# A hybrid encoder layer with product-key experts: the stores of spread weights cut into four pieces, and one row rate for the whole first product

## The chip, the cores and the metric

The kernel runs on one core of a Trainium2 chip. What is measured is the device time of one execution in microseconds (us); the median of the runs shown is compared. The core has a matmul engine (PE, with its weight loads PEld), a vector engine (DVE), a scalar engine (ACT), GpSimd (POOL) and SyncE (SP). SP starts nearly all the plain transfers here, in the order of its own stream, and POOL starts the gathers by index. All transfers share 16 DMA engines.

## The reference

One layer over 1024 tokens of width 1024: a mixer with two groups (RG-LRU and S5), then a product-key retrieval of experts (PEER), then a norm. The change lies in PEER, cut here to what matters:

```python
def block(xb):                                   # 128 tokens
    q = (xb @ wq).reshape(128, 8, 256)           # 8 heads
    s1, s2 = q[..., :128] @ k1.T, q[..., 128:] @ k2.T
    v1, i1 = top_k(s1, 16); v2, i2 = top_k(s2, 16)
    sc, cidx = top_k(v1[..., :, None] + v2[..., None, :], 16)   # of 256 pairs
    e = i1[cidx // 16] * 128 + i2[cidx % 16]     # expert number, 0 .. 16383
    g = softmax(sc)
    act = gelu(einsum('thkd,td->thk', u_tab[e], xb))
    return einsum('thk,thkd->td', g * act, v_tab[e])
```

So each token uses 8 x 16 = 128 of the 16384 experts; u_tab and v_tab are 16384 x 1024 each.

## The kernel before, in words

The eight blocks of 128 tokens are treated in two ways. Five blocks (ND = 5, TD = 640 tokens) are *dense*: the kernel multiplies the 640 tokens with all the experts and weighs the result with a matrix G that holds a token's weight where it chose an expert and zero elsewhere. Three blocks are *gathered*: for each of the 128 experts of a token, POOL fetches the row of u_tab (later of v_tab) by index (`ask`, one gather of 128 rows, 512 KB, a "row" below), and DVE makes one product with it (`row<-row,xg` for u, `hb<-row,act,hb` for v). That is 3 x 256 = 768 rows, taken in order, eight buffers deep.

The dense way has a first product (`first`): for a tile of 128 experts, `ap` = u tile x 640 tokens, in two halves of 320 tokens, each 24 matmuls (every operand is split in a high and a low part: `uh`, `ul`). ACT applies gelu into the tile `aa`, and the 128 x 640 result is stored to DRAM (`A_d<-aa`, 320 KB), to be read back later as `hr`. `ahead` makes 97 such tiles, 194 halves; its buffers are two pairs `uh`/`ul`, and three `aa`. The load of the next u tile is `ur<-in_uT` (512 KB). After them `dense` runs the second product, with the rest of the rows in between; its order is written out by hand.

While `ahead` runs, `choose` finds the experts of the dense blocks (top-k on DVE) and `build` spreads their weights into G: for each group of four tokens, DVE makes the one-hots `ohA` and one part of `ohB`, ACT the rest of `ohB`, PE multiplies them (`gp<-ohB,ohA`), and `flush` copies the result into a buffer `gs` with ACT. One group belongs to one half: 160 groups follow the first 24 halves. A buffer `gs` collects GT = 32 tokens, eight groups. When it is full, `flush` stores it: G_d is laid out by expert tile, so the store of 2 MB writes 128 x 32 runs of 512 bytes. There are two `gs` buffers and 20 such stores. Of the last one, the 64 KB that the first weights load needs (`gt<-G_d`, `weights(0)`) goes first, and the rest (`rest`) in `prologue`, the piece of code that prepares `dense`.

Four things set the order. `Merge`, a planner, runs these generators and always takes the one that is earliest by its own costs. The gathers have a gate: a row may be planned only while `mg.units < allow[0]`; `allow` starts at FIRST, and after LEAD = 23 halves grows by STEP for each half (one value up to half 151, another after it). Then the tile framework sorts each engine's stream again by its own estimate of what is ready, so what the planner wrote is not yet the stream. And SP's stream is a queue: a transfer whose semaphore is not there, or for which the queue has no room, holds all behind it.

Profile lines: everything recorded through the planner has line L146. Before the change the G stores are L1235, the loads of `ur` L1351 (L1537 in `dense`), the stores of `aa` L1449, the loads of `hr` L1381, of `vr` L1385, of `gt` L1486, the gathered block's `hb<-H_d` L1323 and its result `out_dram<-hb` L1346. After the change all but the G stores are three lines further down.

Of the kernel before, what the change touches and what calls it, by code (L numbers as in the profile page):

```python
# [18 lines left out]
P = 128  # L19
# [9 lines left out]
def bc(ap, pos, n):  # L29
    shape = list(ap.shape)  # L30
    v = ap.unsqueeze(pos)
    shape.insert(pos, n)
    return v.to_broadcast(shape)
# [934 lines left out]
TD = ND * P  # L968
HALF = TD // 2
TG = NG * P  # L970
JC = 4
NA = 97
GT = 32
ROWS = 8
PACE = 2.0
FIRST, STEP, KT, LEAD = 64, (1.55, 2.1), 2, 23


def peer(tc, a, cst, pools, h, nx, mg):


    nc = tc.nc
# [9 lines left out]
    G_d = dr.tile([P // JC, P, TD, JC], F32, name="G_d")  # L992
# [202 lines left out]
    rest = []  # L1195
# [28 lines left out]
    def build():  # L1224
        last = None

        def flush():
            gs, b, t4, p_ = last
            S.activation(gs[:, :, t4 % GT:t4 % GT + 4].rearrange("p j t q -> p t j q"),
                         p_.rearrange("p (t j q) -> p t j q", t=4, q=JC), AF.Copy)  # L1230
            if t4 % GT == GT - 4:
                t0 = b * P + t4 + 4 - GT

                def store(js):
                    nc.sync.dma_start(G_d[js, :, t0:t0 + GT].rearrange("j p t q -> p j (t q)"),  # L1235
                                      gs[:, js].rearrange("p j t q -> p j (t q)"))
                if t0 + GT < TD:
                    store(slice(0, P // JC))
                else:
                    store(slice(0, 1))  # L1240
                    weights(0)
                    rest.append(lambda: store(slice(1, P // JC)))
                mg.dma(GT * 64)
        for b, t4 in [(b, t4) for b in dblocks for t4 in range(0, P, 4)]:
            if t4 == 0:
                if f"k{b}" not in mg.flags:
                    yield f"k{b}"
                kt = kts.pop(b)
            yield lambda: steps[0] >= LEAD + groups[0] or "ahead" in mg.flags
            if t4 % GT == 0:  # L1250
                gs = pk2.tile([P, P // JC, GT, JC], F32, name="gs", tag="gs")
            p_ = pb("gp")
            A = pk2.tile([P, 4, P], F32, name="ohA", tag="ohA")
            B = pk2.tile([P, 4, P], F32, name="ohB", tag="ohB")
            V.tensor_tensor(A, bc(iota, 1, 4), bc(kt[:, 0, t4:t4 + 4], 2, P), ALU.is_equal)
            for e in range(4):
                t = t4 + e
                if e:
                    S.activation(B[:, e], iota, AF.Abs, bias=kt[:, 3, t:t + 1])
                else:  # L1260
                    V.tensor_scalar(B[:, e], iota, kt[:, 1, t:t + 1], kt[:, 2, t:t + 1], ALU.is_equal, ALU.mult)
            for e in range(1, 4):
                t = t4 + e
                S.activation(B[:, e], B[:, e], AF.Relu, bias=kt[:, 2, t:t + 1], scale=kt[:, 4, t:t + 1])
            yield lambda: steps[0] >= LEAD + groups[0] + 1 or "ahead" in mg.flags
            for e in range(4):
                PE.matmul(p_[:, e * P:(e + 1) * P], A[:, e], B[:, e], start=True, stop=True)
            if last:
                flush()
            last = gs, b, t4, p_  # L1270
            groups[0] += 1
            yield
        flush()
        mg.flag("g")
        yield
# [97 lines left out]
    class Tile:  # L1373
# [4 lines left out]
        def load_h(self):  # L1378
            if self.hr is None:
                self.hr = ph1.tile([P, TD], F32, name="hr", tag="hr", bufs=3)  # L1380
                nc.sync.dma_start(self.hr, A_d[self.j])  # L1381

        def load_v(self):
            self.vr = pu.tile([P, D], F32, tag="raw", name="vr", bufs=3)
            nc.sync.dma_start(self.vr, a["v"][:, self.j])  # L1385
# [30 lines left out]
    def tile(c, n):  # L1416

        if c >= nch:
            return None
        if (c, n) not in TL:  # L1420
            TL[c, n] = Tile(c * JC + (0, 1, 3, 2)[n])
        return TL[c, n]
# [53 lines left out]

    pace[0] = PACE
    mg.add([(0.0, build()), (0.0, choose()), (1.0, ahead())])
    mg.run([], until="k")
    pools.close("pk")  # L1480
# [3 lines left out]
    def weights(c):  # L1484
        gts[c] = pgg.tile([P, TD, JC], F32, name="gt", tag="gt")
        nc.sync.dma_start(gts[c], G_d[c])  # L1486
# [47 lines left out]
    def load_u(c):  # L1534
        if c < nch:
            raw_u[c] = pu.tile([P, 8, P], F32, tag="raw", name="ur", bufs=3)
            nc.sync.dma_start(raw_u[c], a["uT"][tile(c, 2).j])  # L1537
# [10 lines left out]
    def prologue():  # L1548
        now = [tile(0, n) for n in range(JC)]

        def split_v(n):
            now[n].load_v()
            mg.at(mg.dma(512))
            yield
            now[n].high_v()
            now[n].low_v()
            yield

        def weighted(n):
            now[n].turn()  # L1560
            now[n].weigh()
            yield

        def split_h(n):
            now[n].high_h()
            now[n].low_h()
            yield
        for n in (0, 1):
            yield from split_v(n)
        load_h(0, 0)  # L1570
        load_h(0, 1)
        rest.pop()()
        yield lambda: made[0] >= NA - 2
        for n in (0, 1):
            yield from weighted(n)
            yield from split_h(n)
            if n == 0:
                load_h(0, 3)
        yield from split_v(2)
        load_v(0, 3)  # L1580
        yield from weighted(3)
        yield "ahead"
        yield from weighted(2)
        yield from split_h(2)
        load_h(1, 0)
        load_h(1, 1)
        load_u(2)
        weights(1)
        load_v(1, 0)
        mg.flag("pro")  # L1590

    mg.run([(0.5, prologue())], until="pro")
    share[:] = [0.0]
    assert len(mg.ths) == 1
# [237 lines left out]
```

## Time and profile before

| | |
|---|---|
| median of 3 runs | 2627.03 us (2619.6 to 2630.09) |
| profiled execution | 2629.31 us, span 2627.5 us |
| PE busy | 2502.6 us (95%) |
| DVE busy | 2364.6 us (90%) |
| ACT busy, POOL busy | 1333.2 us, 1118.6 us |
| moved by DMA | 753.30 MB, 287 GB/s over the span |
| G stores | 20 of 2 MB (the last in two parts), L1235, first started at 745.4 us, last at 1466.9 us |
| copies into gs (one for each group) | 160, from 713.8 to 1465.9 us |
| second product begins | about 1516 us |

Times are from the start of the span. The busy shares are means over stages with different limits, so they are read here by stage: the front and the queries to about 680 us, the first product with the spreading of weights from there to about 1466 us, eleven more halves to 1516 us, and then the second product. The profiled execution stands 2.3 us above the median of the runs.

### The profile page before, as it was taken

Reading aid. Unit: us, or ns where it says so; the run is one execution under the profiler, and the core shown is the slowest. Engines: PE = TensorE matmul, PEld = TensorE weight load, DVE = VectorE, ACT = ScalarE, POOL = GpSimd, SP = SyncE. Lnnn points to the kernel's source line nnn. Section 1 sums busy time; section 2 is a strip of 40 time slices with the busy share of each in tenths; the row PEclk is TensorE's granted clock in tenths of the full one; section 3 lists DMA queues with packets and bytes.
Section 4 is the critical chain, followed back from the end, with each engine's and each line's share of the span. In section 5 each row is a group of like instructions: output and inputs, shape, how many; then the busy total and the mean of one; then the engine's idle time right before and its main releaser. Section 6 shows DMA issues by size and latency. Waiting matters only on the chain.

```text
span 2627.5 us, 40651 instructions
## 1 busy us (share of the span) xinstructions
PE 2502.6 (95%) x14623; PEld 2266.1 (86%) x14623; DVE 2364.6 (90%) x4556; ACT 1333.2 (51%) x2402; POOL 1118.6 (43%) x777
## 2 busy tenths in 40 slices
PE   7998999998999999999979999999999999999997
PEld 6776888998999999999979988888888888888885
DVE  7898659998999999999976399999989999999997
ACT  5566434332387777877856543333343434333342
POOL 0000000254455574546765065545545666555550
PEclk9999999998999999999989999999999999999998
DMA  5113124587899999999999699999999999999993
GB/s 177 35 41 105 65 91 134 189 280 284 285 327 354 342 346 325 344 318 343 399 375 378 210 328 359 349 362 353 350 328 349 349 355 356 351 350 353 354 359 116
DMA packets 302538, 753.30 MB, mean 287 GB/s; under 512 B 28928, under 2 KB 127424, under 8 KB 297600
## 3 DMA queue, kind: packets, MB, share of 16 engines
q0 software_dynamic: 110592, 402.70, 41.9%
q1 hardware_dynamic: 186048, 337.85, 36.6%
q10 hardware_dynamic: 5696, 10.15, 1.2%
q8 instruction: 115, 1.88, 0.3%
q14 instruction: 87, 0.71, 0.1%
HBM read 663.44 MB, written 85.98 MB: 285 GB/s over the span
## 4 chain that ended last, share of the span: by engine, by line
PE 60%; DVE 25%; DMA 7%; issue 5%; ACT 2%; POOL 1%; ACTq 0%; SPq 0%; DVEq 0%; POOLq 0%
PE vp L146 26%; PE ap L146 18%; PE total L146 7%; DMA A_d<-aa 3%; DVE hb L146 3%; DVE row L146 3%; PE wop L146 3%; DVE ul L146 2%; PE gp L146 2%; DVE oh L146 2%; DVE ohA L146 2%; PE qp L146 2%; DVE ix L146 1%; DMA xq<-in_x_dram 1%; DVE v L146 1%
## 5 line engine op out<-in xcount | busy, mean ns | idle before, releaser
L1287 POOL DMA_INDIRECT row<-in_peer_u_dram,idx x384 | 561.0, 1461 | 952.9 <-DVE scv L146 474.5
L1287 POOL DMA_INDIRECT row<-in_peer_v_dram,idx x384 | 554.8, 1445 | 465.2 <-DVE hb L146 314.3
L146 PE MATMUL ap<-xDl,uh 128*128 128x320 f32 x2048 | 651.5, 318 | 37.7 <-ACT aa L146 36.1
L146 PE MATMUL ap<-xDh,ul 128*128 128x320 f32 x2048 | 637.6, 311 | 5.1 <-DVE ul L146 5.1
L146 PE MATMUL ap<-xDh,uh 128*128 128x320 f32 x2048 | 637.1, 311 | 0.0
L146 DVE SCALAR_TENSOR_TENSOR hb<-row,act,hb 128x1024 f32<-128x1024 f32 x384 | 491.1, 1279 | 4.8
L146 DVE CUSTOM_DVE_ANT_0 row<-row,xg 128x1024 f32<-128x1024 f32 x384 | 456.6, 1217 | 17.3 <-DMA row<-in_peer_u_dram,idx 15.7
L146 PEld LDWEIGHTS ap<-xDl,uh 128*128 128x128 f32 x2048 | 389.5, 190 | 41.6 <-ACT aa L146 38.2
L146 PE MATMUL vp<-vl,hh 128*128 128x512 f32 x1024 | 401.7, 392 | 10.8 <-DVE h L146 8.6
L146 PE MATMUL vp<-vh,hl 128*128 128x512 f32 x1024 | 401.1, 392 | 0.0
L146 PE MATMUL vp<-vh,hh 128*128 128x512 f32 x1024 | 399.9, 390 | 0.0
L146 PEld LDWEIGHTS ap<-xDh,ul 128*128 128x128 f32 x2048 | 389.7, 190 | 7.0 <-DVE ul L146 5.8
L146 PEld LDWEIGHTS ap<-xDh,uh 128*128 128x128 f32 x2048 | 389.0, 190 | 0.0
L146 ACT ACTIVATE gq<-gt 128x640 f32<-128x640 f32 x128 | 175.1, 1368 | 318.7 <-DVE hr L146 254.7
L146 PEld LDWEIGHTS vp<-vl,hh 128*128 128x128 f32 x1024 | 193.4, 189 | 52.4 <-DVE h L146 9.4
L146 PEld LDWEIGHTS vp<-vh,hh 128*128 128x128 f32 x1024 | 193.4, 189 | 41.2
L146 PEld LDWEIGHTS vp<-vh,hl 128*128 128x128 f32 x1024 | 193.4, 189 | 39.0
L146 ACT ACTIVATE ohB<-ohB,kt 128x128 f32<-128x128 f32 x480 | 202.0, 487 | 0.0
L146 ACT ACTIVATE aa<-ap 128x320 f32<-128x320 f32 x194 | 84.4, 436 | 212.1 <-PE ap L146 165.3
L146 DVE TENSOR_TENSOR ul<-ur,uh 128x1024 fp32r<-128x1024 f32 x128 | 155.7, 1217 | 38.0 <-ACT uh L146 38.0
L146 DVE TENSOR_TENSOR h<-h,vp 128x1024 f32<-128x1024 f32 x128 | 155.5, 1215 | 28.0 <-PE vp L146 27.1
L146 PE MATMUL gp<-ohB,ohA 128*128 128x128 f32 x1280 | 170.3, 276 | 9.3 <-DVE ohB L146 7.0
(444 smaller groups left out, 4484.7 us busy)
## 6 DMA issues: line engine op xcount, KB each, us to landing
ur<-in_uT_dram SPq DMA_DIRECT2D x128, 512.0 KB
vr<-in_peer_v_dram SPq DMA_DIRECT2D x128, 512.0 KB
gt<-G_d SPq DMA_DIRECT2D x32, 1280.0 KB
G_d<-gs SPq DMA_DIRECT2D x19, 2048.0 KB
A_d<-aa SPq DMA_DIRECT2D x96, 320.0 KB
hr<-A_d SPq DMA_DIRECT2D x96, 320.0 KB
wqr<-in_wq_dram SPq DMA_DIRECT2D x31, 512.0 KB
row<-in_peer_u_dram,idx POOLq DMA_INDIRECT x384
```

What stands on the lines that cost most here:

```text
L146: return fn(*args, **kw)
L1287: G.indirect_dma_start(out=r, out_offset=None, in_=a["peer_v" if at >= P else "peer_u"], in_offset=bass.IndirectOffsetOnAxis(ap=idx[n][:, ...
```

## The change

Three edits. The row rate becomes one number: FIRST 72 instead of 64, and 1.6 rows for each half throughout instead of 1.55 up to half 151 and 2.1 after it. Each G store becomes four stores of 8 of the 32 expert tiles each, 512 KB; `flush` only lists them in `rest`, and `build` takes one from the list at each of the next four groups, pinned behind what was already written for SP (`keep_in_program_order`). The last store's four pieces are taken one by one in `prologue`.

```diff
-FIRST, STEP, KT, LEAD = 64, (1.55, 2.1), 2, 23
+FIRST, STEP, KT, LEAD = 72, (1.6, 1.6), 2, 23
...
                 def store(js):
-                    nc.sync.dma_start(G_d[js, :, t0:t0 + GT].rearrange("j p t q -> p j (t q)"),
-                                      gs[:, js].rearrange("p j t q -> p j (t q)"))
-                if t0 + GT < TD:
-                    store(slice(0, P // JC))
-                else:
+                    ins = nc.sync.dma_start(G_d[js, :, t0:t0 + GT].rearrange("j p t q -> p j (t q)"),
+                                            gs[:, js].rearrange("p j t q -> p j (t q)"))
+                    if t0 + GT < TD:
+                        tc.keep_in_program_order(ins)
+                if t0 + GT == TD:
                     store(slice(0, 1))
                     weights(0)
-                    rest.append(lambda: store(slice(1, P // JC)))
+                for c in range(0, P // JC, 8):
+                    rest.append(lambda c=max(c, t0 + GT == TD), e=c + 8: store(slice(c, e)))
...
             yield lambda: steps[0] >= LEAD + groups[0] or "ahead" in mg.flags
+            if rest:
+                rest.pop(0)()
...
         load_h(0, 1)
-        rest.pop()()
+        rest.pop(0)()
         yield lambda: made[0] >= NA - 2
         for n in (0, 1):
             yield from weighted(n)
             yield from split_h(n)
+            rest.pop(0)()
             if n == 0:
                 load_h(0, 3)
         yield from split_v(2)
         load_v(0, 3)
         yield from weighted(3)
+        rest.pop(0)()
+        assert not rest
```

In the built streams the pieces do not stand one group apart. SP's stream at the store that follows the 71st store of `aa`, before:

```order
L1449 DMA A_d<-aa 128x640
L1351 DMA ur<-in_uT_dram 128x1024
L1235 DMA G_d<-gs 128x32x128
L1449 DMA A_d<-aa 128x640
L1346 DMA out_dram<-hb 128x1024
L1351 DMA ur<-in_uT_dram 128x1024
L1323 DMA hb<-H_d 128x1024
L1449 DMA A_d<-aa 128x640
```

and now:

```order
L1349 DMA out_dram<-hb 128x1024
L1452 DMA A_d<-aa 128x640
L1326 DMA hb<-H_d 128x1024
L1354 DMA ur<-in_uT_dram 128x1024
L1452 DMA A_d<-aa 128x640
L1354 DMA ur<-in_uT_dram 128x1024
L1235 DMA G_d<-gs 128x8x128 x3
L1452 DMA A_d<-aa 128x640
L1354 DMA ur<-in_uT_dram 128x1024
L1235 DMA G_d<-gs 128x8x128
```

Three pieces stand where the whole store stood, and the fourth one store of `aa` later; the write and the load of the gathered block (`out_dram<-hb`, `hb<-H_d`) have moved ahead of the pieces. The next four stores have three pieces, a store of `aa`, the fourth piece and then `ur`. Of the 19 whole stores 14 have three and one, four have two and two, and one has one and three.

On DVE, from the 129th `ohA` on, the stretch in which the old table allowed 2.1 rows for a half. Before:

```order
L146 TENSOR_TENSOR ohA<-iota,kt 128x512
L146 TENSOR_TENSOR ul<-ur,uh 128x1024
L146 TENSOR_SCALAR ohB<-iota,kt 128x128
L146 ISA row,act<-row,xg 128x1024
L146 ISA act 128x1
L146 ISA row,act<-row,xg 128x1024
L146 ISA act 128x1
L146 ISA row,act<-row,xg 128x1024
L146 ISA act 128x1
```

and now:

```order
L146 TENSOR_TENSOR ohA<-iota,kt 128x512
L146 TENSOR_SCALAR ohB<-iota,kt 128x128
L146 ISA row,act<-row,xg 128x1024
L146 ISA act 128x1
L146 ISA row,act<-row,xg 128x1024
L146 ISA act 128x1
L146 TENSOR_TENSOR ohA<-iota,kt 128x512
L146 TENSOR_SCALAR ohB<-iota,kt 128x128
L146 ISA row,act<-row,xg 128x1024
L146 ISA act 128x1
L146 ISA row,act<-row,xg 128x1024
L146 ISA act 128x1
```

Two to three rows stand at each group, before and now. Counted over the built stream, the rows that stand on DVE ahead of the n-th `ohA`:

| n | 1 | 9 | 17 | 41 | 81 | 97 | 113 | 121 | 129 | 137 | 145 | 153 |
|---|---|---|---|---|---|---|---|---|---|---|---|---|
| before | 61 | 80 | 95 | 132 | 196 | 221 | 247 | 263 | 282 | 304 | 325 | 342 |
| now | 61 | 81 | 97 | 135 | 201 | 228 | 253 | 263 | 283 | 304 | 325 | 341 |

The planner's table asked for more rows early and fewer late; the stream has at most seven more in between, and the same number from the 121st group on. Rows left for `dense` are 427 instead of 426.

At the end of the spreading, SP before:

```order
L1235 DMA G_d<-gs 128x128
L1235 DMA G_d<-gs 128x31x128
L1486 DMA gt<-G_d 128x2560
L1449 DMA A_d<-aa 128x640 x2
L1351 DMA ur<-in_uT_dram 128x1024
L1381 DMA hr<-A_d 128x640 x2
```

and now:

```order
L1235 DMA G_d<-gs 128x128
L1235 DMA G_d<-gs 128x7x128
L1235 DMA G_d<-gs 128x8x128
L1489 DMA gt<-G_d 128x2560
L1452 DMA A_d<-aa 128x640
L1354 DMA ur<-in_uT_dram 128x1024
L1235 DMA G_d<-gs 128x8x128
L1452 DMA A_d<-aa 128x640
L1235 DMA G_d<-gs 128x8x128
L1384 DMA hr<-A_d 128x640 x2
```

The load `ur` has moved ahead of one store of `aa`, and the last 1 MB of G behind it. On ACT, the first `vh` (a tile of the second product; it waits for the G store there) now stands behind the first `gq`, one `uh` and two more `aa`, instead of ahead of them.

## The prediction

> **What bounds the kernel now.** I read the page first, then the chain of waits in order of time, then a table of stages, and last SP's own stream.
>
> ```profile
> span 2627.5 us, 40651 instructions
> PE 2502.6 (95%) x14623; PEld 2266.1 (86%) x14623; DVE 2364.6 (90%) x4556; ACT 1333.2 (51%) x2402; POOL 1118.6 (43%) x777
> PE 60%; DVE 25%; DMA 7%; issue 5%; ACT 2%; POOL 1%; ACTq 0%; SPq 0%; DVEq 0%; POOLq 0%
> ```
>
> Of the chain in order of time (start, us, what), the pieces that are no plain row of matmuls, and one pair that is:
>
> ```profile
> 1279.82 12.13 DMA out_dram<-hb
> ...
> 1304.05 41.20 DMA A_d<-aa
> ...
> 1352.24 3.52 PE ap L146 x24
> 1355.77 0.89 PE gp L146 x8
> ...
> 1391.57 31.91 DMA A_d<-aa
> ...
> 1466.94 9.73 DMA G_d<-gs
> ...
> 1479.62 4.02 DMA ur<-in_uT_dram
> ```
>
> PE is the bound over all; the change can only touch the stretch of the first product. There one half costs PE 3.52 + 0.89 = 4.41 us. The 160 copies into `gs` run from 713.8 to 1465.9 us (the row of that tile, the first below), 752.1 us for 159 steps of 4.41 = 701 us: 51 us are lost there. The table of stages below it says where (columns: stage, its us, busy us of PE, PEld, DVE, ACT, POOL, PE clock, DMA share, GB/s):
>
> ```profile
> L146 ACT ACTIVATE gs<-gp x160: 579/597/608, 713.8 to 1465.9; 128x512 f32<-128x512 f32 x160
> ```
>
> ```profile
> 760.00:1240.00 480.00, 468.75 (x3360) 462.99 (x3359) 480.00 (x1185) 373.71 (x902) 270.03 (x167) 1.00 0.97 339
> 1240.00:1280.00 40.00, 37.25 (x268) 36.87 (x267) 39.97 (x73) 32.06 (x78) 31.57 (x21) 1.00 1.01 378
> 1280.00:1345.00 65.00, 47.19 (x340) 46.57 (x338) 51.30 (x89) 31.75 (x80) 44.51 (x33) 0.91 1.04 408
> 1345.00:1390.00 45.00, 44.18 (x306) 44.18 (x307) 38.06 (x66) 37.20 (x93) 29.53 (x21) 0.95 0.97 363
> 1390.00:1425.00 35.00, 29.39 (x211) 29.20 (x210) 29.53 (x52) 19.48 (x49) 25.86 (x18) 0.95 1.05 404
> 1425.00:1465.00 40.00, 40.00 (x280) 40.00 (x280) 12.76 (x20) 30.96 (x76) 0.00 (x0) 0.96 0.60 203
> 1465.00:1490.00 25.00, 22.44 (x144) 21.81 (x143) 8.24 (x8) 12.51 (x17) 0.00 (x0) 0.93 0.91 292
> 1550.00:1900.00 350.00, 350.00 (x1713) 301.48 (x1712) 337.32 (x340) 140.70 (x154) 191.33 (x141) 1.00 0.96 353
> ```
>
> Up to 1240 us DVE is busy without a gap (480.00 of 480.00) and sets the pace. From 1280 to 1425 us nobody is full but the DMA engines (shares of 1.04 and 1.05, 408 and 404 GB/s), and PE stands for 17.8 and 5.6 us. Whom it waits for, from 1270 to 1490 us, first for the engines, then for SP's stream:
>
> ```profile
> ACT aa L146 <- DMA A_d<-aa: 41.0, 4, 23.1
> PE ap L146 <- ACT aa L146: 24.2, 3, 17.6
> ACT vh L146 <- DMA G_d<-gs: 3.4, 1, 3.4
> ...
> SPq L1323 <- DMA out_dram<-hb: 10.5, 1, 10.5
> ```
>
> ```profile
> 1301.71 0.37 SPq L1235 DMA_DIRECT2D G_d<-gs  x1
> 1304.05 31.11 SPq L1449 DMA_DIRECT2D A_d<-aa  x1
> 1335.26 0.38 SPq L1351 DMA_DIRECT2D ur<-in_uT_dram  x1
> ...
> 1389.47 0.39 SPq L1235 DMA_DIRECT2D G_d<-gs  x1
> 1391.57 23.25 SPq L1449 DMA_DIRECT2D A_d<-aa  x1
> ```
>
> The store of 2 MB of G leaves SP in 0.37 us, but the small store of `aa` behind it finds no room for 31.11 us and lands after 41.20 us. With three `aa` buffers ACT needs that buffer two tiles later, waits up to 23.1 us for it, and PE waits for ACT.
>
> **The change, part by part.**
>
> *The row rate: 0.* By the table 43 halves would lose 0.5 row each. But the streams that the front shows carry as many rows ahead of the 121st, 129th, 137th, 145th and 153rd `ohA` as before, to within one; in between at most seven more, which come off again. A row costs DVE
>
> ```profile
> L146 DVE CUSTOM_DVE_ANT_0 row<-row,xg 128x1024 f32<-128x1024 f32 x384 | 456.6, 1217 | 17.3 <-DMA row<-in_peer_u_dram,idx 15.7
> ```
>
> 1.22 us, so seven are 8.5 us early that DVE gets back by the 121st group, since it is full all the way. Ends: -2 and +4. The single row more in the second product is 1.22 us on a DVE with 350.00 - 337.32 = 12.7 us of slack in 350: 0.
>
> *Stores of the first 1280 us: 0.* DVE has no gap there, so no store holds it; the 60 more issues take SP some 0.4 us each (the G rows above, 0.37 and 0.39), on a stream that otherwise waits.
>
> *The stores at 1301.7 and 1389.5 us: -7.* The store of `aa` now has three of four pieces ahead of it. If its wait shrinks by a quarter, that is 31.11/4 = 7.8 us off the first, and 23.25/4 = 5.8 us off the second, where PE lost 5.6: 13.4 us together. What is late next is the second store of `aa`, behind the fourth piece. Against it stands the volume: one gather is 402.70 MB / 768 = 0.524 MB (row below), and rows, `ur`, `aa` and G are the same bytes up to the same group. The three stages from 1280 to 1425 us moved 65 x 408 + 45 x 363 + 35 x 404 = 57.0 MB in 145 us; at 408 GB/s all through they would take 139.7, 5.3 us less. The forecast lies nearer to this limit, since no byte goes away, with a little for PE's clock, which reads 0.91 after the stall. Ends: 0, and -23.2 (17.6 + 5.6) if both stops go.
>
> ```profile
> q0 software_dynamic: 110592, 402.70, 41.9%
> ```
>
> *The gathered block's write and load: -1.* SP waited 10.5 us in L1323 for a write that took 12.13 us behind a G store. Now both stand ahead of the pieces and one store of `aa` later than the G store before. PE lost 40 - 37.25 = 2.75 us in that stage. Ends: -4 and +2.
>
> *The end of the spreading: -2.* PE lost 25 - 22.44 = 2.6 us there: ACT's `vh` waited 3.4 us for the G store, the next `aa` came late, SP's next store and the `ur` behind it (4.02 us) too. Now `ur` goes out one store of `aa` earlier and `vh` stands two `aa` later. But `vh` waits for the last piece, which stands behind another store of `aa`; a quarter of 9.73 us is 2.4 us. Ends: -4 and +5. POOL's stream is the same 768 gathers in the same order.
>
> [...]
>
> ```profile
> 1293.38 0.38 SPq L1449 DMA_DIRECT2D A_d<-aa  x1
> 1293.99 0.25 SPq L1351 DMA_DIRECT2D ur<-in_uT_dram  x1
> 1294.33 0.38 SPq L1449 DMA_DIRECT2D A_d<-aa  x1
> ```
>
> SP starts 320 and 512 KB transfers 0.3 to 0.6 us apart without waiting for the one before, so a cost of each piece overlaps; I take 0.
>
> Sum: 0 + 0 - 7 - 1 - 2 = -10 us on the profiled 2629.31: 2619.3. The runs' median is 2.3 us lower, so 2617.
>
> **The rivals.**
>
> *Volume alone decides* (2626). The pieces change the order in the queue, not the bytes, and 1280 to 1425 us is a stretch full of DMA; only the end gains 1 us. For it: shares of 1.04 and 1.05. Against: 363 GB/s in the stage between them, so there is some room.
>
> *Both stops go* (2601). 17.6 + 5.6 + 2.6 of PE's waits and 2 of the clock's recovery end: -28. It needs the `aa` store to land within two tiles, 17.6 us, of a queue that took 41.20. Against: three quarters of 31.11 are still 23.3 us, over the two tiles.
>
> *A new wait makes it slower* (2644). Each transfer of SP carries one of eight completion lanes and waits for the transfer that had it last (the lanes stand among the waits of the built stream). In a window of eight groups, 35 us, nine transfers become thirteen, so a lane returns after 22 us instead of 31. Pieces that land later than that hold SP: at 41 us for four pieces the third is down at 31, some 5 us too late; over the three stores from 1301 us on, 15 us, with no gain elsewhere. It decides when a piece takes over 22 us to land. Against: the queue is first in, first out, and SP would be held there in any case.
>
> *Fixed costs in series* (2650). A 512 KB load took 4.02 us on a quiet queue (above), a quarter of the 2 MB store 2.43: 1.6 us more for each piece, 6.4 for each store, and 20 us over the three stores and the last one where the DMA engines are full. [...]
>
> **How the numbers follow.** What a measurement of this kernel can tell from no change is about 0.5%, 13.1 us: 2613.9 to 2640.2. Chances: the forecast and its neighbourhood 0.47, volume alone 0.20, both stops go 0.20, the new wait 0.08, fixed costs 0.05. The forecast's own spread (its parts' ends taken half way: -7 to -18 and up) crosses 2613.9 in about a third of it, 0.16; with the 0.20 of both stops, faster is 0.36. Volume alone and the other two thirds are same, 0.51; the last two are slower, 0.13. The range leaves out about the outer tenth on each side: from just under 2601 to half way into the slower cases, 2599 to 2636.
>
> **What the profile after would show.** The row rate at nothing: rows from 1280 to 1425 us still some 70 on POOL, DVE full up to 1240 us. The pieces: SP's blocked issue on the second and third piece, the `aa` store landing some 30 instead of 41 us after the first piece, and ACT's wait for `A_d` of 41.0 us down to 20 to 30. The end: `ur` landing before 1480 us and `vh` waiting for G 3 us or less. The prediction is wrong if ACT's wait for `A_d` is nearly gone, if it is as long as before, if PE stops in the first 1280 us for a store, or if SP waits for a piece's landing.

## The result and the profile after

| | before | after |
|---|---|---|
| median, first comparison | 2625.60 us (2616.3 to 2630.1) | 2611.59 us (2602.1 to 2619.0) |
| ratio, with its 95% interval | | 0.9947 (0.9934 to 0.9959) |
| ratio in a second comparison | | 0.9922 (0.9897 to 0.9946) |
| profiled execution, span | 2629.31 us, 2627.5 us | 2613.41 us, 2611.6 us |

The changed kernel is faster by 14 us (10.8 to 17.3), and by 20 us (14 to 27) when it was compared again later. The forecast was 10 us, and its range held the time; but the measured ratio lies just beyond the 0.5% inside which the forecast had put its largest chance.

Not all of the 15.9 us between the two profiled executions is the change. The first copy into `gs` stands at 713.8 us before and at 707.5 after, and up to there the two programs' streams are the same. In the profiles of this study the way from the first matmul of the dense queries to that first copy took from 244.6 to 264.0 us. So I compare lengths of stages, from a copy to a copy, and not times since the start. Of the 15.9 us, 6.4 lie before the first copy, 2.4 in the first 120 groups, 1.2 between the 121st and the 160th copy, 4.6 from there to the second product, and 1.4 in that product. So in this one profile the stretch from which most of the gain was forecast gave 1.2 us; a second profile of the changed kernel (e7) gave 6.1 there.

The head of the page:

```profile
span 2611.6 us, 40763 instructions
PE 2500.6 (96%) x14623; PEld 2264.8 (87%) x14623; DVE 2364.5 (91%) x4556; ACT 1332.7 (51%) x2402; POOL 1137.4 (44%) x777
```

The table of stages, with the windows of the prediction (its columns: stage, its us, busy us of PE, PEld, DVE, ACT, POOL, PE clock, DMA share, GB/s):

```profile
760.00:1240.00 480.00, 467.53 (x3347) 461.43 (x3346) 480.00 (x1201) 374.25 (x900) 277.92 (x169) 1.00 0.97 344
1240.00:1280.00 40.00, 40.00 (x293) 40.00 (x292) 38.98 (x67) 33.40 (x83) 29.19 (x14) 1.00 1.02 366
1280.00:1345.00 65.00, 54.55 (x363) 53.94 (x363) 53.19 (x93) 38.26 (x95) 48.09 (x35) 0.92 1.02 389
1345.00:1390.00 45.00, 44.89 (x326) 44.65 (x325) 43.36 (x78) 35.70 (x90) 36.28 (x26) 1.00 1.04 402
1390.00:1425.00 35.00, 26.03 (x173) 25.52 (x173) 18.15 (x33) 17.41 (x44) 13.93 (x10) 0.85 0.99 363
1425.00:1465.00 40.00, 40.00 (x288) 40.00 (x287) 11.56 (x17) 24.82 (x58) 0.00 (x0) 1.00 0.56 173
1465.00:1490.00 25.00, 25.00 (x173) 25.00 (x172) 10.30 (x10) 14.62 (x19) 0.00 (x0) 1.00 0.84 279
```

PE's gap (a stage's length less PE's busy time) went from 17.8 to 10.5 us between 1280 and 1345 us, but from 5.6 to 9.0 between 1390 and 1425. (The same windows hold work that is 6 to 10 us further on now.) The gap at the end (1465 to 1490) is gone, and with it the lower clock there (0.93 before, 1.00 now). SP's stream at the two stops:

```profile
1296.58 12.09 SPq L1235 DMA_DIRECT2D G_d<-gs  x3
1308.77 4.83 SPq L1452 DMA_DIRECT2D A_d<-aa  x1
1313.65 0.74 SPq L1235 DMA_DIRECT2D G_d<-gs  x1
1314.49 5.24 SPq L1354 DMA_DIRECT2D ur<-in_uT_dram  x1
...
1376.98 17.18 SPq L1235 DMA_DIRECT2D G_d<-gs  x3
1394.26 9.97 SPq L1452 DMA_DIRECT2D A_d<-aa  x1
1404.28 0.48 SPq L1235 DMA_DIRECT2D G_d<-gs  x1
1404.85 4.21 SPq L1354 DMA_DIRECT2D ur<-in_uT_dram  x1
```

SP is now held at the pieces themselves (12.09 and 17.18 us for three issues), and the store of `aa` no longer for 31.11 and 23.25 us but for 4.83 and 9.97. In the chain, the first stop is now a load of `ur` and the second still a store of `aa`:

```profile
1314.49 22.02 DMA ur<-in_uT_dram
...
1394.26 19.17 DMA A_d<-aa
...
1455.97 45.76 PE ap L146 x312
```

At the first stop the store of `aa` lands at 1308.77 + 16.80 = 1325.6 us, 29.0 us after the first piece was started; before it was 1304.05 + 41.20 - 1301.71 = 43.5 us after the whole store. At the second stop it lands at 1394.26 + 19.17 = 1413.4 us, 36.5 us after the first piece; before it was 1391.57 + 31.91 - 1389.47 = 34.0 us. The pieces made nothing earlier there. Whom the engines wait for, 1270 to 1490 us:

```profile
ACT aa L146 <- DMA A_d<-aa: 21.8, 3, 14.6
...
ACT uh L146 <- DMA ur<-in_uT_dram: 11.2, 3, 7.6
...
PE ap L146 <- ACT aa L146: 8.3, 1, 8.3
```

Before, the wait for `ur` was

```profile
ACT uh L146 <- DMA ur<-in_uT_dram: 2.7, 2, 1.4
```

ACT's wait for the stores of `aa` went from 41.0 to 21.8 us, and its wait for `ur` from 2.7 to 11.2. PE's 8.3 us of waiting for `aa` lie all at the second stop, where it was 5.6; at the first, what PE still loses is put down to other engines, and `ur` stands behind it in the chain.

### The profile page after: what moved, and what is told of

Its sections match the earlier page's. It is cut to its first block, busy times and chain, and to the rows that moved or that the text cites. A ratio compares the mean times of both kernels' runs of the same rounds, so it can differ in the third digit from the quotient of the medians.

```text
span 2611.6 us, 40763 instructions
## 1 busy us (share of the span) xinstructions
PE 2500.6 (96%) x14623; PEld 2264.8 (87%) x14623; DVE 2364.5 (91%) x4556; ACT 1332.7 (51%) x2402; POOL 1137.4 (44%) x777
## 4 chain that ended last, share of the span: by engine, by line
PE 67%; DVE 22%; DMA 4%; issue 3%; ACT 2%; POOL 0%; ACTq 0%; DVEq 0%; SPq 0%; POOLq 0%
PE vp L146 26%; PE ap L146 21%; PE total L146 7%; PE qp L146 4%; DVE hb L146 3%; PE gp L146 3%; PE wop L146 3%; DVE ul L146 2%; DVE row L146 2%; DVE ohA L146 2%; DVE oh L146 1%; DVE ci L146 1%; DMA ur<-in_uT_dram 1%; DMA row<-in_peer_u_dram,idx 1%; DVE ix L146 1%
## 5 line engine op out<-in xcount | busy, mean ns | idle before, releaser
L1290 POOL DMA_INDIRECT row<-in_peer_u_dram,idx x384 | 571.8, 1489 | 933.8 <-DVE scv L146 470.2
L1290 POOL DMA_INDIRECT row<-in_peer_v_dram,idx x384 | 562.8, 1466 | 451.4 <-DVE hb L146 304.9
L146 PEld LDWEIGHTS gp<-ohB,ohA 128*128 128x128 f32 x1280 | 161.0, 193 | 26.5 <-issue 13.1
## 6 DMA issues: line engine op xcount, KB each, us to landing
G_d<-gs SPq DMA_DIRECT2D x79, 512.0 KB, 10.7
```

The lines of the kernel that those rows point to most:

```text
L146: return fn(*args, **kw)
L1290: G.indirect_dma_start(out=r, out_offset=None, in_=a["peer_v" if at >= P else "peer_u"], in_offset=bass.IndirectOffsetOnAxis(ap=idx[n][:, ...
```

## The experiments

Two theories. *Order*: PE stops because a small transfer stands behind 2 MB in SP's queue, and the pieces let it pass earlier. *Volume*: in this stretch all transfers together are at the limit of the DMA engines, and order only decides who waits. The measure used is the way from the 121st to the 137th and on to the 153rd copy into `gs`, 16 groups each; without any wait that is 16 x 4.41 = 70.6 us each. A copy stands where ACT comes to it, so the same 16 groups can hold some 20 matmuls of PE more or fewer (the count behind PE's busy time). PE's gap is free of that, and so, nearly, is the way to the 160th copy.

**Each edit alone.** First the rate:

```diff
-FIRST, STEP, KT, LEAD = 64, (1.55, 2.1), 2, 23
+FIRST, STEP, KT, LEAD = 72, (1.6, 1.6), 2, 23
```

> Only the row rate is changed (72, 1.6 and 1.6), all stores as before. The theory that the rate does nothing, because the built streams hold the same number of rows ahead of the 121st to the 153rd group: within 3 us of the kernel before, the waits of ACT for A_d near 41 us as before. The rival that the rate thins the stretch from 1280 to 1425 us and takes the store's stalls away: 8 us or more faster, and ACT's wait for A_d under 25 us.

Measured: 2617.55 us, 0.9977 (0.9958 to 0.9996), some 6 us, between the two expectations; ACT's wait for the stores of `aa` is 28.4 us. Then the 19 stores in pieces (pinned for SP as in the change), with the old rates and the last store as it was:

```diff
                 else:
-                    store(slice(0, P // JC))
+                    for c in range(0, P // JC, 8):
+                        rest.append(lambda c=c, e=c + 8: store(slice(c, e)))
...
+            if rest:
+                rest.pop(0)()
```

> Only the 19 whole stores of G are cut into four pieces; the row rates and the last store are as before. Theory (three quarters ahead of the store of aa instead of all): 3 to 8 us faster, gained between the groups 121 and 153, ACT's wait for A_d near 22 us as in the changed kernel, PE without a gap at the end of the spreading only by chance. Rival, volume alone: within 2 us. Rival, the pieces carry all of the gain: 12 to 16 us faster.

Measured: 2618.24 us, 0.9966 (0.9954 to 0.9979), some 9 us, about the upper end of what the first theory expected. Then only the last store in pieces:

```diff
-                    rest.append(lambda: store(slice(1, P // JC)))
+                    for c in range(0, P // JC, 8):
+                        rest.append(lambda c=max(c, 1), e=c + 8: store(slice(c, e)))
...
+            rest.pop(0)()
...
+        rest.pop(0)()
```

> Only the last store is cut and its pieces taken one by one; the 19 other stores and the rates are as before. Theory from the two profiles (from the last copy into gs to the first matmul of the second product 50.3 us before, 45.7 us after): 4 to 5 us faster, PE without a gap from the last gp on. Rival, the pieces only move the wait of vh: within 2 us.

Measured: 2617.85 us, 0.9969 (0.9956 to 0.9982), some 8 us where 4 to 5 were expected. The kernel before was also run under a label of its own:

> The kernel before once more, unchanged. The first copy into gs came at 713.8 us before and at 707.5 us in the changed kernel, although every engine's stream is the same up to there. Theory, this is the scatter of single executions: the ratio is 1.000 within its interval, and the first copy comes anywhere from 705 to 716 us in this profile and in those of the other three. Rival, it belongs to the kernel before: 713 to 715 us here, and the three others split by their edits.

Measured: 2622.82 us, 0.9997 (0.9986 to 1.0009), against 2625.83 for before in that comparison.

From the 160th copy to the first matmul of the second product took 50.1 us before and 50.2 to 50.8 us in e0, e1 and e2, but 45.6 in e3 and after the change: 4.6 us, and clearly the last store's pieces. The stretch of the two halves, before and with the pieces alone:

```profile
1265.71:1357.09 91.38, 72.75 (x513) 72.14 (x512) 73.11 (x129) 54.37 (x138) 58.98 (x43) 0.91 1.01 389
1357.09:1435.44 78.35, 72.74 (x514) 72.55 (x513) 62.90 (x110) 55.31 (x137) 51.97 (x36) 0.96 1.04 396
```

```profile
1260.19:1341.49 81.30, 73.62 (x518) 73.44 (x516) 70.91 (x125) 55.50 (x137) 57.73 (x42) 0.94 1.04 405
1341.49:1422.79 81.30, 76.60 (x534) 75.38 (x533) 64.49 (x113) 54.40 (x137) 54.86 (x37) 0.98 1.05 406
```

The first half loses 10 us. The second is 3 us longer, but it holds 20 more matmuls (534 against 514), and the seven groups left then take 27.6 us instead of 30.5. From the 121st to the 160th copy it is 190.2 us instead of 200.2, and PE's gap falls from 18.6 to 7.7 us in the first half and from 5.6 to 4.7 in the second. The bytes are nearly the same (91.38 x 389 + 78.35 x 396 = 66.6 MB before, 81.30 x 405 + 81.30 x 406 = 65.9 MB), and with the pieces the DMA engines run at 405 GB/s all through. That 66 MB at this rate need the 163 us that they took says nothing by itself, since the rate was read there. But kernels with unlike orders come to 403 to 406 GB/s over this stretch (e1, e2, e5, e6), and none goes further: that end is volume. The rate alone, in its one profile:

```profile
1260.30:1342.49 82.19, 73.67 (x518) 73.24 (x516) 75.48 (x136) 55.22 (x138) 61.12 (x43) 0.96 1.04 401
1342.49:1419.38 76.89, 72.41 (x515) 72.22 (x513) 61.01 (x107) 54.71 (x137) 50.26 (x35) 0.98 1.05 404
```

159.1 us for 64.0 MB. The rate moves the gathered block's write and load (1.05 MB) and about one gather's bytes out of the stretch; by its stream the block's sum is finished after the 118th group's one-hots instead of the 122nd's. The write starts after the 116th copy into `gs` with the rate alone, and after the 123rd with the pieces alone (the 124th before), so it is not the pieces that move it. SP's wait for it (1250 to 1440 us), with the rate alone and with the pieces alone:

```profile
SPq L1323 <- DMA out_dram<-hb: 5.3, 1, 5.3
```

```profile
SPq L1328 <- DMA out_dram<-hb: 9.1, 1, 9.1
```

The three parts alone add up to 6 + 9 + 8 = 23 us, more than the whole. So:

**Two edits together, and the whole again.** Rate and last store (against the kernel before), then all stores with the old rate (against the changed kernel), then the changed kernel as it is:

```diff
-FIRST, STEP, KT, LEAD = 64, (1.55, 2.1), 2, 23
+FIRST, STEP, KT, LEAD = 72, (1.6, 1.6), 2, 23
...
-                    rest.append(lambda: store(slice(1, P // JC)))
+                    for c in range(0, P // JC, 8):
+                        rest.append(lambda c=max(c, 1), e=c + 8: store(slice(c, e)))
...
```

> The new row rate and the cut last store; the other 19 stores stay whole. Theory A (scatter): the 121st to the 160th copy into gs took 189.6 us with the rate alone and 199.0 us in the changed kernel, and that difference is scatter of single executions. Then the rate is worth its median, -6 us, and the end -5: -9 to -12 us, ratio about 0.996, and that stretch may lie anywhere from 190 to 200 us. Theory B (the rate and the cut stores get in each other's way): the rate really saves 10 us in that stretch as long as the stores are whole. Then it is again 188 to 192 us here, the first product up to there 2 us shorter, the end 4.6 us shorter: -15 to -18 us, ratio 0.993 to 0.9945, as fast as the whole change or faster. Both: from the 160th copy to the second product 45 to 46 us instead of 50.

```diff
-FIRST, STEP, KT, LEAD = 72, (1.6, 1.6), 2, 23
+FIRST, STEP, KT, LEAD = 64, (1.55, 2.1), 2, 23
```

> All four-piece stores, the old row rate. If the parts add up by place (19 stores -9 us by their run, end -4.6): -13 to -14 us, ratio about 0.995, which leaves the rate nothing in the whole change. If the rate gives 2.5 us of the whole change (the first 120 groups), -10 to -12 us, ratio 0.9957. If the single results of the parts were about 3 us too good each: -8 us, 0.997. From the 160th copy to the second product 45 to 46 us in every case; from the first to the 121st copy 552 to 553 us, as with the old rate before.

> The changed kernel unchanged, a second profile and time: ratio 0.9935 to 0.996 as before. Its stretch from the 121st to the 160th copy tells scatter from mechanism: 199 us again (within 2) if the rate and the pieces get in each other's way, or 188 to 196 us if the first profile was an unlucky execution. First to 121st copy 549 to 550 us, 160th copy to the second product 45 to 46 us.

| | us | ratio (interval) | 121st to 137th | 137th to 153rd |
|---|---|---|---|---|
| rate and last store (e4) | 2617.80 | 0.9959 (0.9941 to 0.9978) | 86.1 | 81.2 |
| all stores (e5) | 2615.44 | 0.9953 (0.9935 to 0.9971) | 81.2 | 82.3 |
| all, again (e7) | 2611.02 | 0.9922 (0.9897 to 0.9946) | 82.5 | 81.1 |
| all, first profile | 2611.59 | 0.9947 (0.9934 to 0.9959) | 87.1 | 81.4 |

The time before was 2631.06 us in this comparison and 2625.60 in the last row's. e4 falls by 11 us and not by 15 to 18, and its stretch took 167.3 us with the same stream that took 159.1 in e1: one profile of this stretch scatters by up to 8 us, so theory A of e4's expectation holds and theory B falls. e5 falls by 12 us, its second case. e7's ratio lies a little below the expected 0.9935 to 0.996, and by its way from the 121st to the 160th copy (194.1 us) the first profile of the changed kernel (199.0) was an unlucky execution. When one price for each edit is fitted to all eight ratios, each weighed by its interval, the rate is worth 3.3 us (give or take 3.1), the 19 stores 6.8 (2.5) and the last store 6.4 (2.7), 16.6 together, and no ratio lies more than 1.6 standard errors off. So the edits add up as far as these runs can tell, and the 23 us of the single runs can be scatter.

The profiles show less than the fit. PE's gap, us, in the two halves:

| stores | rate | profiles | 121st to 137th | 137th to 153rd |
|---|---|---|---|---|
| whole | old | before, e0, e3 | 18.6, 16.6, 15.7 | 5.6, 5.4, 5.5 |
| pieces | old | e2, e5 | 7.7, 9.5 | 4.7, 5.2 |
| whole | new | e1, e4 | 8.5, 13.2 | 4.5, 8.1 |
| pieces | new | after, e7 | 10.5, 6.6 | 9.1, 9.8 |

At the old rate the pieces take 6 to 11 us from the first half and the second pays nothing back. At the new rate the two halves together are 13.0 and 21.2 us with whole stores, 19.5 and 16.4 with pieces: no gain can be read there. That the pieces gain in the changed kernel too rests on the fitted times.

**Order without pieces.** The kernel before, with its 19 whole stores started by ACT, so that nothing of SP's stands behind them:

```diff
-                    store(slice(0, P // JC))
+                    nc.scalar.dma_start(G_d[:, :, t0:t0 + GT].rearrange("j p t q -> p j (t q)"),
+                                        gs.rearrange("p j t q -> p j (t q)"))
```

> As before the change, but the 19 whole stores of G are issued from ACT's queue instead of SP's, so that no store of aa and no ur stands behind them; same bytes, whole stores, the last store as before. If the order in SP's queue holds PE: SP's issue of aa behind a G store no longer blocked for 20 to 31 us, ACT's wait for the store of aa under 10 us instead of about 40, the 121st to the 160th copy 185 to 192 us instead of 200, time -8 to -14 us (ratio 0.9945 to 0.997). If the volume alone holds it: the same bytes must pass, that stretch stays at 196 us or more with waits for rows or ur in place of those for aa, and the ratio is 0.999 to 1.002. If the store's issue now holds ACT itself: ACT's queue waits over 5 us a store and the ratio is over 1.002.

Measured: 2627.86 us, 0.9991 (0.9975 to 1.0008): no change. Its halves, ACT's wait that took the place of the old one (1270 to 1490 us), and SP's own (1250 to 1440 us):

```profile
1274.39:1366.47 92.08, 80.00 (x551) 78.88 (x550) 81.22 (x139) 55.10 (x137) 68.83 (x49) 0.96 1.04 408
1366.47:1437.53 71.06, 68.23 (x472) 67.28 (x473) 51.69 (x89) 54.36 (x136) 37.84 (x27) 0.96 1.04 396
```

```profile
ACT gs L146 <- DMA G_d<-gs: 23.5, 3, 11.1
```

```profile
SPq L1352 <- DMA G_d<-gs: 74.8, 4, 27.7
```

The wait for `aa` is gone altogether, as the order theory says, and yet the stretch takes 163.1 us: now the copy into `gs` waits because a G store lands too late, and SP's load of `ur`, which shares no data with G, waits for a G store's landing. The traces show why: the transfers of SP and ACT take their completion semaphores in turn from the same eight (numbers 100 and 102 to 108; all 784 such transfers in the trace of the kernel before carry one of them, and all 844 in that of the changed kernel). The G store that ACT started at 1269.50 us and the `ur` that SP started at 1321.54 both carry number 106, and SP waits for it (27.7 us, the longest of the four waits). So e6 moves the order into the semaphores more than it takes it away, and does not by itself part order from volume. The stretch is 5 to 7 us shorter than before, as with the pieces, and 191.9 us to the 160th copy, which is what the order theory expected; the time is what the volume theory expected. But the framework laid out the streams anew (PE's too), and the first 120 groups took 556.8 us instead of 552, with 15.2 us of PE waiting for `ul` where the kernel before had none of 0.5 us. The price of those groups may be the new order or the second queue; it was not separated.

The other way round, the changed kernel with the stores of `aa` started by ACT, and PE's order as it was:

```diff
-                nc.sync.dma_start(A_d[j], t)
+                nc.scalar.dma_start(A_d[j], t)
```

> The changed kernel with the stores of aa issued from ACT's queue instead of SP's; PE's order of work is unchanged, and so are the bytes. In the changed kernel's two profiles the 121st to the 153rd copy into gs took 168.5 and 163.6 us for 64.7 MB, while the kernel with the rate alone moved the like amount in 159.1 us at 403 GB/s, and five kernels never did it above 406 GB/s. If what is left is SP's queue order (aa and ur behind the pieces), ACT's wait for A_d falls from 22 to 26 us to under 6, that stretch to 158 to 161 us (64.7 MB at 405 GB/s), and the time by 5 to 9 us more: ratio to before 0.990 to 0.992. If the engines' volume holds it in any order, the wait for aa is replaced by one for ur or for rows, the stretch stays at 162 us or more and the ratio at 0.993 to 0.995. If the issues now hold ACT, PE waits for aa or uh by ACT's own queue and the ratio is above 0.995.

Measured: 2621.71 us, 0.9975 (0.9957 to 0.9994), slower than the changed kernel by its ratios of 0.9947 and 0.9922. SP's stream and the wait that came:

```profile
1299.39 29.93 SPq L1235 DMA_DIRECT2D G_d<-gs  x4
1329.43 21.18 SPq L1354 DMA_DIRECT2D ur<-in_uT_dram  x4
```

```profile
ACT uh L146 <- DMA ur<-in_uT_dram: 35.0, 7, 18.2
```

Without the stores of `aa` between them four pieces stand together, SP is held for 29.93 us and four loads of `ur` behind that; ACT waits 35.0 us for `ur` and not at all for `aa`. Neither run with transfers on ACT's queue as well moved more over the stretch than e2 with the stores and loads on SP's queue alone (405 GB/s): e6 came to 403 GB/s over its 163.1 us, its halves at 408 and 396, and e8 to 383 over its 166.1 us, its halves at 381 and 386.

**Less volume.** The changed kernel with fewer rows in the last fifth of the spreading; nothing is left out, 29 rows come later:

```diff
-FIRST, STEP, KT, LEAD = 72, (1.6, 1.6), 2, 23
+FIRST, STEP, KT, LEAD = 72, (1.6, 0.8), 2, 23
```

> The changed kernel with 0.8 instead of 1.6 rows for each half from the 152nd half on: by its stream 29 rows of u, 29 x 0.524 = 15.2 MB, leave the stretch from the 121st to the 160th copy into gs for the second product; nearly all of them stood between the 137th and the 153rd. If volume bounds the stretch, the 137th to the 153rd copy falls from 81 us (both profiles of the changed kernel) towards PE's own 16 x 4.41 = 70.6 us, say 71 to 74, with a DMA share under 0.95, although two stores of G with a store of aa and a ur behind each of them stand there as before. If the order in SP's queue alone holds it, those waits stay: 78 us or more. The 29 rows are 29 x 1.22 = 35 us of DVE in the second product, whose 1110 us have 40 us of slack by the stage 1550 to 1900: if they fit, -7 to -10 us for the whole (ratio 0.990 to 0.992); if DVE becomes the bound there, the second product grows by 5 to 20 us and the ratio is 0.994 to 1.000.

Measured: 2601.93 us, 0.9908 (0.9885 to 0.9931).

```profile
1261.77:1344.53 82.76, 76.40 (x536) 75.74 (x535) 74.00 (x134) 55.34 (x138) 60.13 (x42) 0.96 1.04 398
1344.53:1412.45 67.92, 67.92 (x496) 67.92 (x495) 29.95 (x51) 55.34 (x138) 9.20 (x7) 1.00 0.70 241
...
1550.00:1900.00 350.00, 349.95 (x1720) 301.21 (x1720) 344.02 (x365) 141.16 (x154) 216.25 (x147) 1.00 0.98 367
```

The second half is at PE's own pace, 67.9 us for 496 matmuls, without a gap, although its two G stores, with `aa` and `ur` behind them, stand there as before. The second product took 1110.9 us, against 1110.0 and 1113.5 in the two profiles of the changed kernel, and its DVE went from 338 to 344.02 busy of 350. So at 241 GB/s the same order does no harm: what it costs depends on the volume. (The edit takes DVE's work on these rows away as well; DVE had not been full there, 62.81 of 81.41 us in the changed kernel.)

The same rates with the 19 stores whole (the last in pieces):

```diff
-FIRST, STEP, KT, LEAD = 64, (1.55, 2.1), 2, 23
+FIRST, STEP, KT, LEAD = 72, (1.6, 0.8), 2, 23
...
-                    rest.append(lambda: store(slice(1, P // JC)))
+                    for c in range(0, P // JC, 8):
+                        rest.append(lambda c=max(c, 1), e=c + 8: store(slice(c, e)))
...
```

> The rates 72 and 1.6, then 0.8, with the 19 stores whole as before the change (the last store in four pieces): by its stream again 312 rows ahead of the 153rd group instead of 341. If the pieces help only because the stretch is full of transfers (rows, G, aa, ur), then with 29 rows fewer the whole stores cost little: the 137th to the 153rd copy again 68 to 72 us, the 121st to the 137th perhaps 84 to 92, since that part still holds all its rows; ratio to before 0.991 to 0.994, 0 to 6 us behind the same rates with pieces (0.9908). If the order in SP's queue holds PE by itself, the store of aa behind each whole store still costs its stop of 5 to 18 us at the two stores behind the 137th and 145th group too, that part stays at 76 us or more, and the ratio at 0.995 or more.

Measured: 2604.54 us, 0.9927 (0.9904 to 0.9951).

```profile
1266.16:1352.21 86.05, 73.53 (x518) 73.10 (x516) 75.45 (x136) 55.45 (x138) 60.36 (x43) 0.92 1.04 396
1352.21:1422.82 70.61, 70.61 (x514) 70.61 (x513) 28.75 (x49) 55.67 (x137) 7.62 (x6) 1.00 0.64 218
```

A whole 2 MB store costs PE nothing in the second half (70.61 of 70.61); the store of `aa` behind it is held for 2.38 us, not for 23 to 31. In the first half, still full of rows, PE's gap is 12.5 us with whole stores and 6.4 with pieces, and both halves together, with the same number of matmuls, take 6.0 us more with whole stores. So in these two profiles, one of each, the pieces of the 19 stores pay only where the DMA engines are full (the first half, a share of 1.04 in both, against 0.70 and 0.64 in the second). By the ratios they are worth 5 us at these rates, within intervals that overlap.

One step further:

```diff
-FIRST, STEP, KT, LEAD = 72, (1.6, 1.6), 2, 23
+FIRST, STEP, KT, LEAD = 72, (1.5, 0.9), 2, 23
```

> The changed kernel with 1.5 rows for a half up to the 151st and 0.9 after it: by its stream 5 rows fewer ahead of the 97th group and 38 fewer ahead of the 153rd than the changed kernel has (9 fewer than with 1.6 and 0.8). The first 120 groups, where DVE has no gap, should not change by more than 6 us (rows 263 ahead of the 121st as before, 6 fewer ahead of the 113th); the 137th to the 153rd copy at PE's pace, 68 to 71 us. 38 x 1.22 = 46 us of DVE then go into a second product that had 40 us of room: if DVE becomes the bound there, the second product takes 1115 to 1125 us instead of 1111 and the ratio is 0.992 to 0.996; if it still fits, 0.987 to 0.991.

Measured: 2621.03 us, 0.9978 (0.9960 to 0.9996), beyond the slower of the two cases expected. The second half is at 69.9 us, but the second product takes 1123.4 us and the first 120 groups 553.2 (549.1 with 1.6 and 0.8):

```profile
1550.00:1900.00 350.00, 348.23 (x1699) 298.63 (x1699) 344.47 (x379) 141.38 (x155) 223.31 (x152) 1.00 0.98 372
```

PE now has a gap there (348.23 of 350) with DVE at 344.47. PE's wait for DVE over the whole second product, in e15 and here:

```profile
PE vp L146 <- DVE h L146: 4.7, 4, 2.5
```

```profile
PE vp L146 <- DVE h L146: 12.6, 15, 4.2
```

Nine rows past the best version the room in the second product is used up. The 4 us more in the first 120 groups come with the slower rate up to half 151; nothing here takes them apart.

## Why the prediction was right, and where it was not

*The number.* 2617 was forecast and 2611.6 measured. The sum of the terms was -10 us; the fit gives -16.6, and the two comparisons -14 and -20.

*The row rate: 0 forecast, -3.3 (give or take 3.1) measured.* This term failed. I wrote that rows, `ur`, `aa` and G are the same bytes up to the same group. They nearly are, but between the 121st and the 153rd copy the changed kernel moves 87.09 x 385 + 81.41 x 383 = 64.7 MB, 1.9 MB less than before:

```profile
1257.00:1344.09 87.09, 76.64 (x525) 76.03 (x524) 74.25 (x134) 55.32 (x138) 67.02 (x42) 0.94 1.02 385
1344.09:1425.50 81.41, 72.33 (x506) 71.58 (x505) 62.81 (x109) 54.52 (x137) 50.92 (x36) 0.94 1.02 383
```

The step that failed is the one from equal rows to equal bytes. It left out the gathered block's own write and load, which SP's order ahead of the prediction shows moved, and which I put down to the pieces. It is the rate that moves them (above). What it is worth shows most clearly ahead of that stretch: from the 117th to the 121st copy PE's gap is 2.0 us in the five profiles with the old rate (before, e0, e2, e3, e5) and 0.0 in the six with 72 and 1.6 on SP's queue alone, and the first 120 groups took 549.1 to 550.8 us with these against 551.9 to 553.1. (Their DVE does about one row and one pair of one-hots less between these two copies; whether that is saved, or done ahead of the first copy, the scatter in front of it hides.) Whether the 1.9 MB gain more in the stretch itself is not shown: with whole stores and the new rate it took 159.1 us once and 167.3 once.

*The 19 stores: -7, with -1 for the block; measured -6.8 (2.5).* The size was right by the fit, and its reason, the limit by bytes, is the one that e15 and e16 bear out: I took 5.3 us from 57.0 MB at 408 GB/s. By the profiles it is less sure. At the old rate the way from the 121st to the 160th copy falls from 198.9 to 200.2 us (before, e0, e3) to 190.2 and 191.0 (e2, e5), 8 to 10 us, with the stretch at 405 and 406 GB/s; in the changed kernel it is 199.0 and 194.1. So that the -7 was met so closely is partly luck. The -1 for the block came, but from the rate. The quarter off each stop held at the first alone: PE's gap fell by 17.8 - 10.5 = 7.3 us, where 7.8 was worked out. The second did not fall: PE's gap there is 4.7 and 5.2 us with the pieces at the old rate (5.4 to 5.6 without), and 9.1 and 9.8 at the new one. Since it is 8.1 in e4 too, with whole stores, the growth is not shown to come from the pieces, and its cause stays open. That the `ur` behind the fourth piece would be next, I did not say; I named the second store of `aa`.

*The end: -2 forecast, 4.6 us less in the profiles, -6.4 (2.7) by the fit.* The mechanism was right (the gap of 2.6 us is gone, `vh` still waits 3.0 us but behind two more `aa`, and `ur` lands at 1469.1 us), but the term counted only the gap. The clock read 0.93 over 25 us and now reads 1.00, 25 x 0.07 = 1.8 us more by estimate; 2.6 + 1.8 = 4.4 of the 4.6.

*The rivals.* Volume alone: it does set the floor, as e15 and e16 show, but the kernel before stood some 5 us above it (66.6 MB at 405 GB/s are 164.4 of its 169.7 us), and at the old rate the pieces took that. The changed kernel, with 64.7 MB and so 159.8 us, still stands 4 and 9 us above its own floor (163.6 and 168.5); what holds it there is not shown beyond the waits for `aa` and `ur`. Both stops go: they did not. A new wait: with the pieces at the old rate SP waits once for a G piece's landing, 5.7 us in e2 from 1250 to 1440 us, and in the first profile of the changed kernel never. Fixed costs in series: at the first stop SP started three pieces at 1296.58, 1297.06 and 1299.34 us, before the first of them landed at 1312.12; the 79 pieces of 512 KB land after 10.7 us in the median, the first 120 groups take no longer with pieces (553.1 and 552.0 us in e2 and e5, 551.9 to 552.7 with whole stores and the old rate), and in the full stretch after them e2 and e5 move 405 and 406 GB/s, where whole stores at that rate move 392 to 394. None of these numbers shows time lost to a cost of each piece. Two slips of the working change no chance: volume alone is priced on the runs' median and the other three rivals on the profiled time, 2.3 us higher, and a piece down at 31 us is 9 and not 5 us behind a lane that returns after 22.

*The signs named.* POOL's rows from 1280 to 1425 us are 71 (72 before), DVE is full to 1240 us, SP is held at the pieces, ACT's wait for `aa` is 21.8 us (26.1 in the second profile): as said. The store of `aa` landing some 30 us after the first piece: so at the first stop, 29.0 us, and not at the second, 36.5.

## What to carry to other kernels

In the stretch that was full of transfers here (a DMA share of 1.02 and 1.04 in its halves), cutting the big store let small ones go out sooner: the longest issue of a store of `aa` fell from 31.1 to 10.0 us. At the old rate the way from the 121st to the 153rd copy became 6 to 7 us shorter (169.7 us before, 162.6 and 163.5 in e2 and e5), where its 66.6 MB at 405 GB/s had left some 5; so in another kernel work that distance out first, in MB and GB/s, with every transfer that moves. Then look at what the next stop does. Moving bytes to a stage that has room gained as well: with 29 rows later this kernel took 2601.9 us, 24 us less than before and, by the ratios, 4 to 10 less than with the change under study. Nine rows more, with a slower rate ahead of them, threw most of it away.

## What the runs showed of the hardware

The row of `aa`'s stores, before and after (shortest, median and longest issue in ns): one such issue on SP was held up to 31.1 us behind a whole store, and in the changed kernel at most 10.0.

```profile
L1449 SPq DMA_DIRECT2D A_d<-aa x96: 319/327/31109, 620.2 to 1502.7; - x96
```

```profile
L1452 SPq DMA_DIRECT2D A_d<-aa x96: 319/327/9967, 617.8 to 1488.2; - x96
```

Gathers, loads and stores of 512-byte runs together came to 403 to 406 GB/s over some 160 us in four kernels with unlike orders (e1, e2, e5, e6), and no kernel here went higher over such a stretch. A store started from ACT's queue held up SP's next load of other data for 27.7 us, where both carry the same one of the eight completion semaphores (e6). Of the 706 landings that the trace of the changed kernel holds for SP's transfers, none is out of the order in which SP started them.
